# Fixing by hand the order of the last 15 microseconds of a streaming prefix-sum kernel

## The chip, the cores and the metric

The kernel runs on one core of a Trainium2 chip. The metric is the device time in microseconds (us); lower is better. The profile's "span" (first to last instruction) is about 1.7 us shorter than the time.

Names in the profile: PE is the matmul engine TensorE, PEld its weight loads, DVE is VectorE, ACT is ScalarE, POOL is GpSimd, SP is the engine that issues the loads. L218 is a line of the kernel.

## The reference

```python
B, H, W = 4, 4224, 4224          # x: float32
ps   = np.cumsum(np.cumsum(x, axis=1), axis=2)
diag = np.diagonal(ps, axis1=1, axis2=2)
return np.cumsum(diag, axis=1)   # [4, 4224]
```

Only the diagonal of the two-dimensional prefix sum is wanted. Its step from row i-1 to row i is the sum of row i up to the diagonal plus the sum of column i above it. The kernel computes these steps and takes two prefix sums of them.

## The kernel before

Each of the four matrices is read in 33 blocks of 128 rows, 2.1 MB a load, six buffers. For block I, ScalarE sums the rows up to the diagonal block's end, VectorE makes a masked product of the diagonal block and adds the rest to an accumulator, and TensorE turns the masked product and the accumulator's slice into column sums.

```python
for I in range(NB):                                   # NB = 33
    ...
    nc.sync.dma_start(out=xt, in_=x[b, P*I : P*(I+1), :])
    nc.scalar.activation(out=act_scratch[:, 0:P*(I+1)], in_=xt[:, 0:P*(I+1)],
                         func=Copy, accum_out=rp_full[:, I:I+1])          # row sums
    nc.vector.tensor_tensor_reduce(out=du, in0=xt[:, P*I:P*(I+1)], in1=u_strict,
                         ..., accum_out=rp_du[:, I:I+1])                  # masked product
    nc.tensor.matmul(cp_ps[:, I:I+1], lhsT=du, rhs=ones_col, ...)         # column sums
    nc.tensor.matmul(cp_ps[:, I:I+1], lhsT=acc[:, P*I:P*(I+1)], rhs=ones_col, ...)
    nc.vector.tensor_tensor(out=acc[:, P*(I+1):], in0=acc[:, P*(I+1):],
                         in1=xt[:, P*(I+1):], op=add)
```

The last matrix has a tail of its own. The steps of 31 blocks go through the prefix sums while the last two blocks still arrive; the block before the last (31) is loaded in two parts, the last (32) in four chunks; what these two blocks add is put on top by small matmuls.

```python
    # block 31: ScalarE sums columns 0..2304, VectorE the 1792 others
    # block 32: ScalarE sums all four chunks (1408, 1152, 1152, 512 columns)
tt(s31, rp_full[31], rp_du[31], subtract); tt(s31, s31, cp_ps[31], add)
nc.vector.tensor_copy(out=s31mat[:, 31:32], in_=s31)
nc.tensor.matmul(ot_ps[0:32, :], lhsT=s31mat, rhs=ramp_ut, ...)           # rows 0..31
nc.tensor.matmul(ot_ps[32:33, :], lhsT=s31, rhs=ramp_full, ...)
nc.vector.tensor_copy(ot_sb[0:32, :], ot_ps[0:32, :])                     # 32-row copy
nc.gpsimd.dma_start(out=..., in_=ot_sb[0:32, :])
    # five dependent 128x1 additions on VectorE:
    #   pre = part0 + part1; pre += part2; pre2 = pre - rp_du; pre2 += cp_ps; delta = pre2 + part3
nc.tensor.matmul(ot_ps[32:33, :], lhsT=delta, rhs=ramp_ut, ...)           # the last matmul
nc.scalar.copy(ot_sb[32:33, :], ot_ps[32:33, :])
nc.scalar.dma_start(out=..., in_=ot_sb[32:33, :])                         # the last output
```

(`tt` is short for a VectorE addition or subtraction. `s31` holds the steps of block 31, `s31mat` the same as the last column of a matrix of zeros, and `delta` the steps of block 32.) In what order VectorE works through all this is left to the program's scheduler.

## Time and profile before

| before | |
|---|---|
| time, median of 12 runs | 682.93 us (682.72 to 683.09) |
| span of the profiled run | 681.2 us |
| loads | 285.48 MB |
| last chunk told landed (the last of its 16 semaphore updates in the trace) | 673.5 us |
| start of the last matmul | 677.9 us |

The first fence has lines of the page of the kernel before. Slices are fortieths of the span; a digit is the busy share in tenths.

```profile
span 681.2 us, 2484 instructions
DMA  8999999999999999999999999999999999999993
q1 hardware_dynamic: 19584, 285.48, 98.6%
q8 instruction: 4, 0.07, 0.0%
q14 instruction: 9, 0.07, 0.0%
DMA 82%; DVE 9%; ACT 5%; PE 2%; issue 1%; SPq 0%; DVEq 0%; ACTq 0%
```

The DMA engines are full from the second slice to the last but one: the loads bind. (The last line is the chain of waits by engine: 82% of it is DMA.) At about 429 GB/s the bytes alone take 665 us. A change of the tail can therefore touch only what lies after the stream.

The second fence is the timeline of the tail of the kernel before: start, duration, engine, line, operation; in brackets the idle time just before and what ended it.

```profile
671.37 2.00 DVE L218 TENSOR_REDUCE rp_parts<-xt 128x1 f32<-128x1792 f32 x1
673.30 0.27 DVE L238 CUSTOM_DVE_ANT_0 du<-xt,u_strict 128x128 f32<-128x128 f32 x1
673.63 0.59 PE L248 MATMUL cp_ps<-ones_col,du 128*128 128x1 f32 x2 [1.50 <-DVE rp_du L238]
673.78 0.27 DVE L238 CUSTOM_DVE_ANT_0 du<-xt,u_strict 128x128 f32<-128x128 f32 x1
674.55 0.18 ACT L190 ACTIVATION_READ_ACCUMULATOR act_scratch<-xt 128x1 f32 x1
675.54 0.15 DVE L299 TENSOR_TENSOR s<-s,cp_ps 128x1 f32<-128x1 f32 x1 [1.41 <-PE cp_ps L258]
675.94 0.42 PE L306 MATMUL ot_ps<-ramp_ut,s31mat 128*32 128x128 f32 x1 [0.43 <-DVE s31mat L305]
676.62 0.28 DVE L322 COPY ot_sb<-ot_ps 32x128 f32<-32x128 f32 x1 [0.74 <-PE ot_ps L314]
677.72 0.16 DVE L346 TENSOR_TENSOR delta<-pre,rp_parts 128x1 f32<-128x1 f32 x1
677.94 0.59 PE L354 MATMUL ot_ps<-ramp_ut,delta 128*1 128x128 f32 x2 [1.37 <-DVE delta L346]
678.56 0.26 ACT L362 COPY ot_sb<-ot_ps 1x128 f32<-1x128 f32 x1 [3.83 <-PE ot_ps L354]
678.85 0.50 ACTq L363 DMA_DIRECT2D out_dram<-ot_sb  x1
```

Both masked products (the two L238 lines) stand behind the 2.00 us reduce, although their data had landed earlier. TensorE sits idle for them, and VectorE then sits idle 1.41 us for the column sums. ScalarE had its last row sum at 674.7 (L190). From there to 677.9 everybody waits for a chain of small operations.

### The profile page before, as it was taken

The numbers are of one execution on the slowest core, as the hardware profiler recorded it, in microseconds if no ns is written. First come the engines' busy times: TensorE is split into PE (matmuls) and PEld (weight loads), VectorE is DVE, ScalarE is ACT, GpSimd is POOL, SyncE is SP. The second block draws the span as 40 slices with busy tenths as digits, with TensorE's granted clock in tenths as the row PEclk, the third lists the DMA queues.
The fourth block names the chain that finished last, engine by engine and source line by source line (L and its number), as shares of the span: only waits on it lengthen the run. The fifth ranks groups of instructions, "written<-read, shape, count | busy, mean of one in ns | idle before, by whom it ended". The sixth has DMA issues, their size and how long they took to land.

```text
span 681.2 us, 2484 instructions
## 1 busy us (share of the span) xinstructions
PE 146.1 (21%) x590; PEld 129.2 (19%) x590; DVE 330.3 (48%) x440; ACT 279.1 (41%) x272; POOL 4.0 (1%) x16
## 2 busy tenths in 40 slices
PE   0121121121321211211232211212123112112124
PEld 0121121121211211211221111212112112112112
DVE  3876553221587664421177755533118866544213
ACT  1122344567312333555712223445661123345565
POOL 1000000000000000000000000000000000000000
DMA  8999999999999999999999999999999999999993
GB/s 365 433 429 429 429 429 428 428 429 428 428 428 430 429 428 427 429 429 429 427 430 429 429 427 427 429 429 429 429 429 429 429 428 429 429 429 429 429 422 136
DMA packets 19727, 285.69 MB, mean 419 GB/s; under 512 B 2256, under 2 KB 2306, under 8 KB 2946
## 3 DMA queue, kind: packets, MB, share of 16 engines
q1 hardware_dynamic: 19584, 285.48, 98.6%
q8 instruction: 4, 0.07, 0.0%
q0 software_dynamic: 128, 0.07, 0.0%
q14 instruction: 9, 0.07, 0.0%
q10 hardware_dynamic: 2, 0.00, 0.0%
HBM read 285.47 MB, written 0.07 MB: 419 GB/s over the span
## 4 chain that ended last, share of the span: by engine, by line
DMA 82%; DVE 9%; ACT 5%; PE 2%; issue 1%; SPq 0%; DVEq 0%; ACTq 0%
DMA xt<-in_x_dram 82%; DVE acc L273 6%; ACT act_scratch L230 5%; DVE acc L269 1%; DVE du L238 1%; PE cs_ps L110 0%; PE ot_ps L114 0%; PE cs_ps L101 0%; DVE rp_parts L218 0%; DVE p_sb L96 0%; DVE a_sb L96 0%; PE p_ps L106 0%; PE p_ps L119 0%; SPq L185 0%; PE cp_ps L248 0%
## 5 line engine op out<-in xcount | busy, mean ns | idle before, releaser
L230 ACT ACTIVATE act_scratch<-xt 128x128 bf16<-128x128 f32 (+10 forms) x130 | 258.9, 1991 | 393.9 <-DMA xt<-in_x_dram 393.9
L273 DVE TENSOR_TENSOR acc<-acc,xt 128x3968 f32<-128x3968 f32 (+30 forms) x124 | 283.5, 2286 | 0.0
L238 DVE CUSTOM_DVE_ANT_0 du<-xt,u_strict 128x128 f32<-128x128 f32 x132 | 38.4, 291 | 318.4 <-DMA xt<-in_x_dram 318.4
L248 PE MATMUL cp_ps<-ones_col,du 128*128 128x1 f32 x264 | 77.3, 362 | 514.5 <-DVE rp_du L238 514.4
L248 PEld LDWEIGHTS cp_ps<-ones_col,du 128*128 128x128 f32 x264 | 66.2, 311 | 527.2 <-DVE rp_du L238 517.5
L258 PE MATMUL cp_ps<-ones_col,acc 128*128 128x1 f32 x256 | 72.4, 352 | 0.0
L258 PEld LDWEIGHTS cp_ps<-ones_col,acc 128*128 128x128 f32 x256 | 69.9, 333 | 0.0
L230 ACT ACTIVATION_READ_ACCUMULATOR act_scratch<-xt 128x1 f32 x130 | 24.2, 186 | 0.0
L238 DVE DVE_READ_ACCUMULATOR2_ANT rp_du<- 128x1 f32 x132 | 10.8, 82 | 0.1
L269 DVE COPY acc<-xt 128x4096 f32<-128x4096 f32 x4 | 9.1, 2276 | 0.0
L281 DVE TENSOR_TENSOR s_sb<-rp_full,rp_du 128x33 f32<-128x33 f32 x3 | 0.6, 195 | 10.5 <-ACT act_scratch L230 10.5
L101 PE MATMUL cs_ps<-s_sb,u_incl 128*128 128x33 f32 x8 | 2.5, 412 | 11.7 <-DVE s_sb L284 8.9
L190 ACT ACTIVATE act_scratch<-xt 128x1152 bf16<-128x1152 f32 (+2 forms) x4 | 4.3, 1074 | 1.2 <-DMA xt<-in_x_dram 1.1
L290 POOL DMA_DIRECT2D out_dram<-ot_sb x3 | 1.7, 573 | 513.3 <-DVE rp_du L238 513.3
L96 DVE COPY a_sb<-a_ps 33x1 f32<-33x1 f32 x8 | 1.2, 151 | 6.6 <-PE a_ps L103 3.4
L101 PEld LDWEIGHTS cs_ps<-s_sb,u_incl 128*128 128x128 f32 x8 | 2.0, 312 | 12.0 <-DVE s_sb L284 9.2
L114 PE MATMUL ot_ps<-u_incl,t_sb 128*33 128x128 f32 x8 | 2.5, 422 | 1.1 <-DVE t_sb L96 1.1
L110 PE MATMUL cs_ps<-p_sb,u_incl 1*128 1x33 f32 x8 | 2.5, 408 | 1.1 <-DVE p_sb L96 1.1
L123 PE MATMUL ot_ps<-u_incl,p_sb 1*33 1x128 f32 x8 | 2.5, 417 | 0.3 <-DVE p_sb L96 0.3
L96 DVE COPY p_sb<-p_ps 1x33 f32<-1x33 f32 x8 | 1.4, 181 | 2.3 <-PE p_ps L106 1.4
L110 PEld LDWEIGHTS cs_ps<-p_sb,u_incl 1*128 1x128 f32 x8 | 2.0, 307 | 1.8 <-DVE p_sb L96 1.8
L96 DVE COPY t_sb<-cs_ps 128x33 f32<-128x33 f32 x4 | 0.8, 194 | 2.9 <-PE cs_ps L110 2.9
(52 smaller groups left out, 23.9 us busy)
## 6 DMA issues: line engine op xcount, KB each, us to landing
xt<-in_x_dram SPq DMA_DIRECT2D x130, 2112.0 KB, 27.1
xt<-in_x_dram SPq DMA_DIRECT2D x1, 1152.0 KB, 24.9
xt<-in_x_dram SPq DMA_DIRECT2D x2, 576.0 KB, 24.8
xt<-in_x_dram SPq DMA_DIRECT2D x1, 960.0 KB, 26.8
xt<-in_x_dram SPq DMA_DIRECT2D x1, 704.0 KB, 23.8
xt<-in_x_dram SPq DMA_DIRECT2D x1, 256.0 KB, 20.4
out_dram<-ot_sb POOLq DMA_DIRECT2D x3, 16.5 KB, 5.7
out_dram<-ot_sb POOLq DMA_DIRECT2D x1, 16.0 KB, 1.7
```

The lines of the kernel that those rows point to most:

```text
L96: nc.vector.tensor_copy(dst, src)
L101: nc.tensor.matmul(cs_ps, lhsT=u_incl, rhs=x_sb, start=True, stop=False)
L110: nc.tensor.matmul(cs_ps, lhsT=ones_row, rhs=p_sb, start=False, stop=True)
L114: nc.tensor.matmul(ot_ps, lhsT=t_sb, rhs=u_incl, start=True, stop=False)
L123: nc.tensor.matmul(ot_ps, lhsT=p2_sb, rhs=ones_row, start=False, stop=True)
L190: nc.scalar.activation(out=act_scratch[:, c0:c1], in_=xt[:, c0:c1], func=mybir.ActivationFunctionType.Copy, accum_out=rp_parts[:, ci : ci ...
L230: nc.scalar.activation(out=act_scratch[:, 0 : P * (I + 1)], in_=xt[:, 0 : P * (I + 1)], func=mybir.ActivationFunctionType.Copy, accum_out= ...
L238: nc.vector.tensor_tensor_reduce(out=du, in0=xt[:, P * I : P * (I + 1)], in1=u_strict, scale=1.0, scalar=0.0, op0=mybir.AluOpType.mult, op ...
L248: nc.tensor.matmul(cp_ps[:, I : I + 1], lhsT=du, rhs=ones_col, start=False, stop=False, skip_group_check=True,)
L258: nc.tensor.matmul(cp_ps[:, I : I + 1], lhsT=acc[:, P * I : P * (I + 1)], rhs=ones_col, start=False, stop=False, skip_group_check=True,)
L269: nc.vector.tensor_copy(out=acc[:, P * (I + 1) :], in_=xt[:, P * (I + 1) :])
L273: nc.vector.tensor_tensor(out=acc[:, P * (I + 1) :], in0=acc[:, P * (I + 1) :], in1=xt[:, P * (I + 1) :], op=mybir.AluOpType.add,)
```

## The change

Intent: fix the order of the tail by hand and shorten its last chain. The first 130 loads and all blocks but the last two stay as they are, in the same order on every engine. In the tail, four things change: (1) the masked products and column sums go ahead of the reduce; (2) the last chunk's sum (512 columns) moves from ScalarE to VectorE; (3) the 32-row copy moves from VectorE to ScalarE; (4) the diagonal terms are folded in early, so that four additions are left instead of five, and none stands behind the copy. The split of block 31 moves from column 2304 to 2432. The core of the new tail, cut:

```diff
+        with tc.manual_schedule(engines={DVE, PE, Activation}):
+            for ci, (c0, c1) in enumerate(last_chunks[: NPART - 1]):
+                nc.scalar.activation(... accum_out=rp_parts[:, ci : ci + 1])   # three chunks
+            ...                                          # prefix sums of 31 blocks, pass 1
+            du31 = masked_product(IL, xt31)
+            accumulate(IL, xt31)
+            t_sb = psum_to_sbuf("t_sb", cs_ps)
+            ...
+            duL = masked_product(LAST, xtL)
+            a2_sb = psum_to_sbuf("a2_sb", a2_ps)
+            colsum(IL, du31);  colsum(IL, acc[...]);  colsum(LAST, duL);  colsum(LAST, acc[...])
+            nc.tensor.matmul(p2_ps, lhsT=a2_sb, ...)
+            nc.vector.reduce_sum(out=part(NPART), in_=xt31[:, sp31 : P * (IL + 1)], ...)
+            tt(s31, part(NPART), part(NPART + 1))
+            p2_sb = psum_to_sbuf("p2_sb", p2_ps)
+            nc.tensor.matmul(ot_ps, lhsT=p2_sb, rhs=ones_row, start=False, stop=True)
+            tt(neg2, cp_ps[:, IL : LAST + 1], rp_du[:, IL : LAST + 1], SUB)
+            tt(s31mat[:, 31:32], s31, neg2[:, 0:1])
+            tail_matmul(slice(0, 32), s31mat, ramp_ut, True)
+            tail_matmul(slice(LAST, LAST + 1), s31mat[:, 31:32], ramp_full, False)
+            nc.vector.reduce_sum(out=part(NPART - 1), in_=xtL[:, d0:d1], ...)  # last chunk
+            tt(fold, part(0), part(1))
+            tt(fold, fold, neg2[:, 1:2])
+            tt(rest, fold, part(2))
+            nc.scalar.copy(ot_sb[0:LAST, :], ot_ps[0:LAST, :])                 # 32-row copy
+            tt(delta, rest, part(NPART - 1))
```

More of the change, by code (lines that the diff above doesn't have):

```diff
@@ L11 @@
 BF16 = mybir.dt.bfloat16
+ACT_COPY = mybir.ActivationFunctionType.Copy
+ACT_IDENT = mybir.ActivationFunctionType.Identity
+ADD = mybir.AluOpType.add
+SUB = mybir.AluOpType.subtract
+MULT = mybir.AluOpType.mult
 @with_exitstack
@@ L81 @@
         c_c = rem - c_b
-        sizes = [c_a, c_b, c_c, c_d]
-        assert all(s >= P for s in sizes) and sum(sizes) == W
         last_chunks = [
@@ L89 @@
         ]
-    else:
+        sp31 = min((W * 3 // 5) // P * P, P * (LAST - 1))
+        fast_tail = 0 < sp31 < P * (LAST - 1)
+    if not fast_tail:
         last_chunks = [(0, W)]
+        sp31 = 0
     NPART = len(last_chunks)
@@ L139 @@
         ot_sb = smalls.tile([NB, P], FP32, name="ot_sb")
-        if last_batch:
-            s31mat = smalls.tile([P, 32], FP32, name="s31mat")
-            nc.vector.memset(s31mat, 0.0)
-            pre = smalls.tile([P, 1], FP32, name="pre")
-            pre2 = smalls.tile([P, 1], FP32, name="pre2")
-            delta = smalls.tile([P, 1], FP32, name="delta")
-            s31 = smalls.tile([P, 1], FP32, name="s31")
-        for I in range(NB):
-            if last_batch and I == LAST - 1:
-                nc.vector.tensor_tensor(
-                    out=s_sb[:, 0 : LAST - 1],
-                    in0=rp_full[:, 0 : LAST - 1],
-                    in1=rp_du[:, 0 : LAST - 1],
-                    op=mybir.AluOpType.subtract,
-                )
-                nc.vector.tensor_tensor(
-                    out=s_sb[:, 0 : LAST - 1],
-                    in0=s_sb[:, 0 : LAST - 1],
-                    in1=cp_ps[:, 0 : LAST - 1],
-                    op=mybir.AluOpType.add,
-                )
-                nc.vector.memset(s_sb[:, LAST - 1 : LAST + 1], 0.0)
-                t_sb = cumsum_pass1(s_sb)
-                cumsum_pass2_transposed(t_sb, ot_ps)
-            split31 = last_batch and I == LAST - 1 and NPART > 1
-            chunked = last_batch and I == LAST and NPART > 1
-            split31_cols = min((P * I * 3 // 5) // P * P, P * I) if split31 else 0
-            xt = tiles.tile([P, W], FP32, name="xt")
-            if chunked:
-                for (c0, c1) in last_chunks:
-                    nc.sync.dma_start(
-                        out=xt[:, c0:c1], in_=x[b, P * I : P * (I + 1), c0:c1]
-                    )
-            elif split31 and 0 < split31_cols < W:
-                nc.sync.dma_start(
-                    out=xt[:, 0:split31_cols],
-                    in_=x[b, P * I : P * (I + 1), 0:split31_cols],
-                )
-                nc.sync.dma_start(
-                    out=xt[:, split31_cols:],
-                    in_=x[b, P * I : P * (I + 1), split31_cols:],
-                )
-            else:
-                nc.sync.dma_start(out=xt, in_=x[b, P * I : P * (I + 1), :])
-            act_scratch = scratch.tile([P, W], BF16, name="act_scratch")
-            if chunked:
-                for ci, (c0, c1) in enumerate(last_chunks):
-                    nc.scalar.activation(
-                        out=act_scratch[:, c0:c1],
-                        in_=xt[:, c0:c1],
-                        func=mybir.ActivationFunctionType.Copy,
-                        accum_out=rp_parts[:, ci : ci + 1],
-                    )
-                    if ci == 1:
-                        nc.vector.tensor_tensor(
-                            out=pre,
-                            in0=rp_parts[:, 0:1],
-                            in1=rp_parts[:, 1:2],
-                            op=mybir.AluOpType.add,
-                        )
-                    elif 1 < ci < NPART - 1:
-                        nc.vector.tensor_tensor(
-                            out=pre,
-                            in0=pre,
-                            in1=rp_parts[:, ci : ci + 1],
-                            op=mybir.AluOpType.add,
-                        )
-            elif split31:
-                half = split31_cols
-                nc.scalar.activation(
-                    out=act_scratch[:, 0:half],
-                    in_=xt[:, 0:half],
-                    func=mybir.ActivationFunctionType.Copy,
-                    accum_out=rp_parts[:, NPART : NPART + 1],
-                )
-                nc.vector.reduce_sum(
-                    out=rp_parts[:, NPART + 1 : NPART + 2],
-                    in_=xt[:, half : P * (I + 1)],
-                    axis=mybir.AxisListType.X,
-                )
-                nc.vector.tensor_tensor(
-                    out=rp_full[:, I : I + 1],
-                    in0=rp_parts[:, NPART : NPART + 1],
-                    in1=rp_parts[:, NPART + 1 : NPART + 2],
-                    op=mybir.AluOpType.add,
-                )
-            else:
-                nc.scalar.activation(
-                    out=act_scratch[:, 0 : P * (I + 1)],
-                    in_=xt[:, 0 : P * (I + 1)],
-                    func=mybir.ActivationFunctionType.Copy,
-                    accum_out=rp_full[:, I : I + 1],
-                )
@@ L237, with load_block, diag_and_colparts @@
+        def load_block(I, ranges=None):
+            xt = tiles.tile([P, W], FP32, name="xt")
+            if ranges is None:
+                ranges = [(0, W)]
+            for (c0, c1) in ranges:
+                nc.sync.dma_start(
+                    out=xt[:, c0:c1], in_=x[b, P * I : P * (I + 1), c0:c1]
+                )
+            return xt
+        def diag_and_colparts(I, xt):
             du = dupool.tile([P, P], FP32, name="du")
@@ L243 @@
                 scalar=0.0,
-                op0=mybir.AluOpType.mult,
-                op1=mybir.AluOpType.add,
+                op0=MULT,
+                op1=ADD,
                 accum_out=rp_du[:, I : I + 1],
@@ L265, with accumulate, row_part @@
                 )
-            if I < NB - 1:
-                if I == 0:
-                    nc.vector.tensor_copy(
-                        out=acc[:, P * (I + 1) :], in_=xt[:, P * (I + 1) :]
-                    )
-                else:
-                    nc.vector.tensor_tensor(
-                        out=acc[:, P * (I + 1) :],
-                        in0=acc[:, P * (I + 1) :],
-                        in1=xt[:, P * (I + 1) :],
-                        op=mybir.AluOpType.add,
-                    )
-        if not last_batch:
-            nc.vector.tensor_tensor(
-                out=s_sb, in0=rp_full, in1=rp_du, op=mybir.AluOpType.subtract
-            )
-            nc.vector.tensor_tensor(
-                out=s_sb, in0=s_sb, in1=cp_ps, op=mybir.AluOpType.add
-            )
+        def accumulate(I, xt):
+            if I >= NB - 1:
+                return
+            if I == 0:
+                nc.vector.tensor_copy(
+                    out=acc[:, P * (I + 1) :], in_=xt[:, P * (I + 1) :]
+                )
+            else:
+                nc.vector.tensor_tensor(
+                    out=acc[:, P * (I + 1) :],
+                    in0=acc[:, P * (I + 1) :],
+                    in1=xt[:, P * (I + 1) :],
+                    op=ADD,
+                )
+        def row_part(I, xt):
+            act_scratch = scratch.tile([P, W], BF16, name="act_scratch")
+            nc.scalar.activation(
+                out=act_scratch[:, 0 : P * (I + 1)],
+                in_=xt[:, 0 : P * (I + 1)],
+                func=ACT_COPY,
+                accum_out=rp_full[:, I : I + 1],
+            )
+        n_plain = NB - 2 if last_batch else NB
+        for I in range(n_plain):
+            xt = load_block(I)
+            row_part(I, xt)
+            diag_and_colparts(I, xt)
+            accumulate(I, xt)
+        if not last_batch:
+            nc.vector.tensor_tensor(out=s_sb, in0=rp_full, in1=rp_du, op=SUB)
+            nc.vector.tensor_tensor(out=s_sb, in0=s_sb, in1=cp_ps, op=ADD)
             t_sb = cumsum_pass1(s_sb)
@@ L291 @@
             continue
-        nc.vector.tensor_tensor(
-            out=s31,
-            in0=rp_full[:, LAST - 1 : LAST],
-            in1=rp_du[:, LAST - 1 : LAST],
-            op=mybir.AluOpType.subtract,
-        )
-        nc.vector.tensor_tensor(
-            out=s31,
-            in0=s31,
-            in1=cp_ps[:, LAST - 1 : LAST],
-            op=mybir.AluOpType.add,
-        )
-        nc.vector.tensor_copy(out=s31mat[:, 31:32], in_=s31)
-        nc.tensor.matmul(
-            ot_ps[0:32, :],
-            lhsT=s31mat,
-            rhs=ramp_ut,
-            start=False,
-            stop=True,
-            skip_group_check=True,
-        )
@@ L314 @@
-        nc.tensor.matmul(
-            ot_ps[LAST : LAST + 1, :],
-            lhsT=s31,
-            rhs=ramp_full,
-            start=False,
-            stop=False,
-            skip_group_check=True,
-        )
-        nc.vector.tensor_copy(ot_sb[0:LAST, :], ot_ps[0:LAST, :])
-        nc.gpsimd.dma_start(
-            out=out_by_block[b, 0:LAST, :], in_=ot_sb[0:LAST, :]
-        )
-        if NPART == 1:
-            base_ap = rp_full[:, LAST : LAST + 1]
-        elif NPART == 2:
-            base_ap = rp_parts[:, 0:1]
-        else:
-            base_ap = pre
@@ L333 @@
-        nc.vector.tensor_tensor(
-            out=pre2,
-            in0=base_ap,
-            in1=rp_du[:, LAST : LAST + 1],
-            op=mybir.AluOpType.subtract,
-        )
-        nc.vector.tensor_tensor(
-            out=pre2,
-            in0=pre2,
-            in1=cp_ps[:, LAST : LAST + 1],
-            op=mybir.AluOpType.add,
-        )
-        if NPART > 1:
-            nc.vector.tensor_tensor(
-                out=delta,
-                in0=pre2,
-                in1=rp_parts[:, NPART - 1 : NPART],
-                op=mybir.AluOpType.add,
-            )
-        else:
-            delta = pre2
+        IL = LAST - 1
@@ new lines @@
+        s31mat = smalls.tile([P, 32], FP32, name="s31mat")
+        nc.vector.memset(s31mat, 0.0)
+        neg31 = smalls.tile([P, 1], FP32, name="neg31")
+        vs31 = smalls.tile([P, 1], FP32, name="vs31")
+        s31 = smalls.tile([P, 1], FP32, name="s31")
+        negL = smalls.tile([P, 1], FP32, name="negL")
+        fold = smalls.tile([P, 1], FP32, name="fold")
+        rest = smalls.tile([P, 1], FP32, name="rest")
+        delta = smalls.tile([P, 1], FP32, name="delta")
+        xt31 = load_block(IL, [(0, sp31), (sp31, W)])
@@ new lines, with masked_product @@
+        xtL = load_block(LAST, last_chunks)
+        nc.vector.memset(s_sb[:, IL : LAST + 1], 0.0)
+        act_scratch = scratch.tile([P, W], BF16, name="act_scratch")
+        nc.scalar.activation(
+            out=act_scratch[:, 0:sp31],
+            in_=xt31[:, 0:sp31],
+            func=ACT_COPY,
+            accum_out=rp_parts[:, NPART + 1 : NPART + 2],
+        )
+        neg2 = smalls.tile([P, 2], FP32, name="neg2")
+        def masked_product(I, xt):
+            du = dupool.tile([P, P], FP32, name="du")
+            nc.vector.tensor_tensor_reduce(
+                out=du, in0=xt[:, P * I : P * (I + 1)], in1=u_strict,
+                scale=1.0, scalar=0.0, op0=MULT, op1=ADD,
+                accum_out=rp_du[:, I : I + 1],
+            )
+            return du
@@ new lines, in colsum, with tail_matmul, tt @@
+        def colsum(I, lhsT):
+            nc.tensor.matmul(
+                cp_ps[:, I : I + 1], lhsT=lhsT, rhs=ones_col,
+                start=False, stop=False, skip_group_check=True,
+            )
+        def tail_matmul(rows, lhsT, rhs, stop):
+            nc.tensor.matmul(
+                ot_ps[rows, :], lhsT=lhsT, rhs=rhs,
+                start=False, stop=stop, skip_group_check=True,
+            )
+        def tt(o, a, c, op=ADD):
+            nc.vector.tensor_tensor(out=o, in0=a, in1=c, op=op)
@@ new lines, in part @@
+        def part(k):
+            return rp_parts[:, k : k + 1]
+        with tc.manual_schedule(
+            engines={mybir.EngineType.DVE, mybir.EngineType.PE, mybir.EngineType.Activation}
+        ):
+            for ci, (c0, c1) in enumerate(last_chunks[: NPART - 1]):
+                nc.scalar.activation(
+                    out=act_scratch[:, c0:c1],
+                    in_=xtL[:, c0:c1],
+                    func=ACT_COPY,
+                    accum_out=rp_parts[:, ci : ci + 1],
+                )
+            tt(s_sb[:, 0:IL], rp_full[:, 0:IL], rp_du[:, 0:IL], SUB)
+            tt(s_sb[:, 0:IL], s_sb[:, 0:IL], cp_ps[:, 0:IL])
+            cs_ps = psum_ph2.tile([P, NB], FP32, name="cs_ps")
+            nc.tensor.matmul(cs_ps, lhsT=u_incl, rhs=s_sb, start=True, stop=False)
+            a_ps = psum_ph2.tile([NB, 1], FP32, name="a_ps", tag="aux_ps")
+            nc.tensor.matmul(a_ps, lhsT=s_sb, rhs=ones_col, start=True, stop=True)
+            a_sb = psum_to_sbuf("a_sb", a_ps)
+            p_ps = psum_ph2.tile([1, NB], FP32, name="p_ps", tag="aux_ps")
+            nc.tensor.matmul(
+                p_ps, lhsT=a_sb, rhs=u_strict[0:NB, 0:NB], start=True, stop=True
+            )
+            p_sb = psum_to_sbuf("p_sb", p_ps)
+            nc.tensor.matmul(cs_ps, lhsT=ones_row, rhs=p_sb, start=False, stop=True)
+            du31 = masked_product(IL, xt31)
+            accumulate(IL, xt31)
+            t_sb = psum_to_sbuf("t_sb", cs_ps)
+            nc.tensor.matmul(ot_ps, lhsT=t_sb, rhs=u_incl, start=True, stop=False)
+            a2_ps = psum_ph2.tile([NB, 1], FP32, name="a2_ps", tag="aux_ps")
+            nc.tensor.matmul(a2_ps, lhsT=t_sb, rhs=ones_col, start=True, stop=True)
+            duL = masked_product(LAST, xtL)
+            a2_sb = psum_to_sbuf("a2_sb", a2_ps)
+            colsum(IL, du31)
+            colsum(IL, acc[:, P * IL : P * (IL + 1)])
+            colsum(LAST, duL)
+            colsum(LAST, acc[:, P * LAST : P * (LAST + 1)])
+            p2_ps = psum_ph2.tile([1, NB], FP32, name="p2_ps", tag="aux_ps")
+            nc.tensor.matmul(
+                p2_ps, lhsT=a2_sb, rhs=u_strict[0:NB, 0:NB], start=True, stop=True
+            )
+            nc.vector.reduce_sum(
+                out=part(NPART),
+                in_=xt31[:, sp31 : P * (IL + 1)],
+                axis=mybir.AxisListType.X,
+            )
+            tt(s31, part(NPART), part(NPART + 1))
[5 more added lines that the diff above has]
+            tail_matmul(slice(LAST, LAST + 1), s31mat[:, 31:32], ramp_full, False)
+            d0, d1 = last_chunks[NPART - 1]
+            nc.vector.reduce_sum(
+                out=part(NPART - 1), in_=xtL[:, d0:d1], axis=mybir.AxisListType.X
+            )
+            tt(fold, part(0), part(1))
[3 more added lines that the diff above has]
+            tt(delta, rest, part(NPART - 1))
@@ L354 @@
+        nc.gpsimd.dma_start(out=out_by_block[b, 0:LAST, :], in_=ot_sb[0:LAST, :])
         nc.tensor.matmul(
```

## The prediction

> **What bounds the kernel now.** The input stream. The page's queue part shows 285.48 MB on the load queue, 98.6% of 16 engines' span; its slices show 427 to 433 GB/s from the second slice on, and the chain of waits gives DMA 82%. (The Trainium skill, "Perfetto Trace Analysis", section "Roofline", puts the 16 DMA engines of a single active core at about 435 GB/s; this trace agrees, 429.) At 429 GB/s the bytes alone take 665 us of the 681.2 us span. The change doesn't touch the 130 whole-block loads; the instruction order of both programs is the same on every engine until the last two blocks. So only what lies after the stream can move. By the packet records the last input packet ends at 673.0 us, and its landing is told at 673.5. The tail after it is 7.7 us, 1.1% of the span: under 2% is certain unless the stream itself breaks.
>
> **The tail now** (timeline of the last 15 us). VectorE works in an order the scheduler chose: the small prefix copies first, then a 1792-wide reduce (671.4 to 673.4, 2.00 us), and only then both masked products of the last two blocks (673.3, 673.8). The four column-sum matmuls therefore run 673.6 to 675.5, s31 at 675.5, its two tail matmuls 675.9 to 676.6, the 32-row copy on VectorE 0.28, then five dependent 128x1 additions from 676.8 to 677.9, about 0.2 us each, the last matmul 677.94, the ScalarE copy 678.56, and the output's issue at 678.85. ScalarE had finished the last chunk at 674.7, so all from there is this chain. Issue to the end of the span: 2.3 us, unchanged.
>
> **After the change, same durations.** s_sb until p_sb stays where it was (666.9 to 669.05). The masked products fit into waits of VectorE at 669.1 and 670.1 (chunk of the last block told by then), so the column sums run at 670.7 to 672.4. The reduce, now 1664 wide (estimate 1.87 us by width), runs 670.95 to 672.8; s31, p2 copy, neg2, s31mat to 673.65. The 512-wide reduce moves from ScalarE (0.61 + 0.19) to VectorE: estimate 0.65, from 673.65 to 674.3. Four additions of 0.2: delta ready at 675.1. Meanwhile the p2 matmul and two tail matmuls end at about 674.6, and ScalarE's 32-row copy ends at 674.9, just before delta, which matters because the last matmul now waits for it too. Last matmul 675.2, ScalarE copy 675.8, issue 676.1. Against 678.85 that is 2.7 us. The 32-row output, issued by GpSimd after 675.0, took 1.7 us to land, and stays hidden.
>
> The removed and added work is nearly equal in size (DVE gains the 0.65 reduce, loses the 0.28 copy and one addition); the gain is order, not work. All of it is on the critical path, since nothing else is left to do after the stream.
>
> **Predicted: 680.2 us**, 8 in 10 between 679.2 and 681.4. Faster by over 2%: 0.005; within 2%: 0.99; slower: 0.005.
>
> **What would show it.** Right: slices and GB/s unchanged to the last; last input packet near 673.0; column sums of the last two blocks start near 670.7; the last ScalarE copy near 675.8; the span near 678.4; VectorE nearly gapless from 671 to 675 and the chain of waits at its end going through its two reduces. Wrong: the column sums still after 673; the last matmul waiting on ScalarE's 32-row copy by over 0.3 us; the issue later than 677.
>
> **What would make it wrong.** From 670.8 to 673.0 only one of the 16 DMA engines still works (DMA share 0.06): if this straggler ends a microsecond earlier or later, because the split at column 2432 instead of 2304 changes packet sizes, the time follows, as VectorE's last reduce waits for it. A small-operation latency 0.1 us longer in each of some eight dependent steps would eat 0.8 us.

## The result, and the profile after

The median is 680.32 us (679.75 to 680.52, 10 runs) against 682.93 us (12 runs): 2.6 us or 0.4% less. The ratio is 0.9961, 95% interval 0.9952 to 0.9970. The prediction was 680.2 us.

Lines of the page of the changed kernel:

```profile
span 678.6 us, 2479 instructions
DMA  8999999999999999999999999999999999999994
q1 hardware_dynamic: 19584, 285.48, 99.0%
DMA 85%; DVE 8%; ACT 5%; PE 1%; issue 1%; SPq 0%; DVEq 0%; ACTq 0%
```

The stream is the same. The timeline of its tail, columns as above:

```profile
669.30 0.27 DVE L252 CUSTOM_DVE_ANT_0 du<-xt,u_strict 128x128 f32<-128x128 f32 x1
670.40 0.29 DVE L252 CUSTOM_DVE_ANT_0 du<-xt,u_strict 128x128 f32<-128x128 f32 x1
670.98 0.59 PE L260 MATMUL cp_ps<-ones_col,du 128*128 128x1 f32 x2
671.16 1.87 DVE L316 TENSOR_REDUCE rp_parts<-xt 128x1 f32<-128x1664 f32 x1
673.49 0.16 DVE L272 TENSOR_TENSOR s31mat<-s,neg 128x1 f32<-128x1 f32 x1
673.86 0.69 DVE L329 TENSOR_REDUCE rp_parts<-xt 128x1 f32<-128x512 f32 x1 [0.21 <-DMA xt<-in_x_dram]
674.69 0.25 ACT L335 COPY ot_sb<-ot_ps 32x128 f32<-32x128 f32 x1 [0.23 <-PE ot_ps L266]
675.10 0.16 DVE L272 TENSOR_TENSOR delta<-rest,rp_parts 128x1 f32<-128x1 f32 x1
675.41 0.59 PE L338 MATMUL ot_ps<-ramp_ut,delta 128*1 128x128 f32 x2 [0.77 <-DVE delta L272]
676.03 0.26 ACT L346 COPY ot_sb<-ot_ps 1x128 f32<-1x128 f32 x1 [1.09 <-PE ot_ps L338]
676.32 0.49 ACTq L347 DMA_DIRECT2D out_dram<-ot_sb  x1
```

The column sums start at 671.0 instead of 673.6, beside the reduce instead of behind it. s31mat is ready at 673.65 instead of 675.9. VectorE now waits 0.21 us for the last chunk: the tail has become so short that the landing of the last load is what its end hangs on. The chain of waits of the changed kernel shows the same: it is DMA until 673.83, then the 512-column reduce, the additions and the last matmul.

```profile
653.48 20.36 DMA xt<-in_x_dram
673.86 0.69 DVE rp_parts L329
675.10 0.17 DVE delta L272
675.41 0.60 PE ot_ps L338 x2
676.03 0.26 ACT ot_sb L346
```

A useful measure for all runs below, since the landing itself moves from run to run, is the time from "last chunk told landed" to "start of the last matmul". It was 677.94 - 673.49 = 4.45 us before and 675.41 - 673.83 = 1.58 us after. The rest, from the last matmul to the end of the span, is unchanged at 3.2 us. Of this, 2.3 us lie between the start of the last output's issue and the end (678.85 to 681.2 before, 676.32 to 678.6 after). The Trainium skill, "DMA: Bandwidth & Descriptors", section "Anatomy of one DMA", puts the fixed cost of a DMA issued from GpSimd at about 2.0 us; here GpSimd's 32-row output landed 1.7 us after its issue. The last output is issued by ScalarE: its landing was told 1.1 us after the start of the issue (at 677.41), and the span ended 1.2 us after that.

### The profile page after: what moved, and what is told of

Its sections match the earlier page's. It is cut to its first block, busy times and chain, and to the rows that moved or that the text cites. A ratio compares the mean times of both kernels' runs of the same rounds, so it can differ in the third digit from the quotient of the medians.

```text
span 678.6 us, 2479 instructions
## 1 busy us (share of the span) xinstructions
PE 145.9 (22%) x590; PEld 129.3 (19%) x590; DVE 330.3 (49%) x438; ACT 278.9 (41%) x271; POOL 4.0 (1%) x16
## 4 chain that ended last, share of the span: by engine, by line
DMA 85%; DVE 8%; ACT 5%; PE 1%; issue 1%; SPq 0%; DVEq 0%; ACTq 0%
DMA xt<-in_x_dram 85%; DVE acc L195 6%; ACT act_scratch L204 5%; DVE acc L191 1%; DVE du L159 1%; PE cs_ps L116 0%; PE ot_ps L120 0%; PE cs_ps L107 0%; SPq L152 0%; DVE p_sb L102 0%; DVE rp_parts L329 0%; DVE a_sb L102 0%; PE ot_ps L338 0%; PE p_ps L112 0%; PE p_ps L125 0%
## 5 line engine op out<-in xcount | busy, mean ns | idle before, releaser
L281 ACT ACTIVATE act_scratch<-xt 128x1152 bf16<-128x1152 f32 (+1 forms) x3 | 3.7, 1234 | 1.0 <-DMA xt<-in_x_dram 0.9
L242 ACT ACTIVATE act_scratch<-xt 128x2432 bf16<-128x2432 f32 x1 | 2.2, 2212 | 0.0
## 6 DMA issues: line engine op xcount, KB each, us to landing
xt<-in_x_dram SPq DMA_DIRECT2D x130, 2112.0 KB, 27.1
```

The source lines that it names most:

```text
L242: nc.scalar.activation(out=act_scratch[:, 0:sp31], in_=xt31[:, 0:sp31], func=ACT_COPY, accum_out=rp_parts[:, NPART + 1 : NPART + 2],)
L281: nc.scalar.activation(out=act_scratch[:, c0:c1], in_=xtL[:, c0:c1], func=ACT_COPY, accum_out=rp_parts[:, ci : ci + 1],)
```

## The experiments

Twelve kernels were run; all gave correct results. "Landed" is when the last chunk was told landed, "last matmul" when it started, both in the profiled run. Each was timed in five rounds with the kernel before on the same chip, the 120-row run in three.

| run | median us | ratio to before (95%) | landed | last matmul | between |
|---|---|---|---|---|---|
| before | 682.93 | | 673.49 | 677.94 | 4.45 |
| after | 680.32 | 0.9961 (0.9952-0.9970) | 673.83 | 675.41 | 1.58 |
| order undone | 681.87 | 0.9985 (0.9972-0.9997) | 673.68 | 677.01 | 3.33 |
| last chunk on ScalarE | 680.11 | 0.9960 (0.9948-0.9973) | 673.67 | 675.25 | 1.58 |
| copy on VectorE | 680.46 | 0.9963 (0.9951-0.9976) | 673.62 | 675.20 | 1.58 |
| order alone | 680.79 | 0.9968 (0.9954-0.9982) | 673.54 | 675.87 | 2.33 |
| order and chain | 680.29 | 0.9962 (0.9948-0.9975) | 673.65 | 675.14 | 1.49 |
| half of TensorE's instructions | 680.91 | 0.9972 (0.9959-0.9984) | 674.39 | 675.97 | 1.58 |
| new tail, first try | 680.77 | 0.9969 (0.9955-0.9982) | 673.54 | 675.61 | 2.07 |
| first try and half of TensorE's | 681.80 | 0.9984 (0.9971-0.9998) | 674.71 | 676.88 | 2.17 |
| 120 and 8 rows | 683.88 | 1.0010 (0.9995-1.0025) | 677.36 | 679.00 | 1.64 |
| fewer VectorE instructions | 678.63 | 0.9938 (0.9925-0.9952) | 672.15 | 673.73 | 1.58 |
| new tail, mended | 680.44 | 0.9965 (0.9952-0.9977) | 673.41 | 674.90 | 1.49 |
| mended and fewer VectorE | 678.88 | 0.9942 (0.9929-0.9954) | 672.26 | 673.71 | 1.45 |

The intervals are about as wide as 1.8 us, so a difference of half a microsecond between two runs is not settled by them. Where the text below rests on so small a difference, it leans on the timeline, and says whether the single times overlap.

### What of the change was worth what

Theory A: the order is the gain. Rival B: the work moved between VectorE and ScalarE is.

**Order undone.** The changed kernel with products and column sums behind the reduce. (The last chunk's reduce and the first addition also move ahead, into VectorE's wait for the column sums; this is not in the cut.)

```diff
-            du31 = masked_product(IL, xt31); accumulate(IL, xt31)     # ahead of t_sb
-            duL = masked_product(LAST, xtL)                           # ahead of a2_sb
-            colsum(IL, ...) x2;  colsum(LAST, ...) x2                 # ahead of the reduce
+            p2_sb = psum_to_sbuf("p2_sb", p2_ps); ...
             nc.vector.reduce_sum(out=part(NPART), in_=xt31[:, sp31 : P * (IL + 1)], ...)
+            du31 = ...; accumulate(...); duL = ...; colsum x4
```

> The changed kernel with one thing undone: the two masked products and the four column-sum matmuls are put back behind the 1664-wide reduce; the last chunk's sum stays on VectorE and the 32-row copy on ScalarE. Theory A (the gain is the order: the column sums no longer wait for the reduce): the reduce runs 671.5 to 673.4, the column sums 673.7 to 675.5, the tail matmuls from 675.9, and the last issue comes at about 678, so the span is 1.7 us longer than the changed kernel's (about 682.0 us, ratio to before near 0.9985). Rival B (the gain is the work moved between VectorE and ScalarE, not the order): it stays within 0.4 us of 680.3.

Measured: 681.87 us, 1.55 us worse than the changed kernel, with no overlap of single times (681.58 and more against 680.52 and less). Its timeline shows the same waits as before the change:

```profile
671.58 1.86 DVE L311 TENSOR_REDUCE rp_parts<-xt 128x1 f32<-128x1664 f32 x1
673.71 0.59 PE L260 MATMUL cp_ps<-ones_col,du 128*128 128x1 f32 x2 [1.37 <-DVE rp_du L252]
675.61 0.16 DVE L272 TENSOR_TENSOR neg<-cp_ps,rp_du 128x2 f32<-128x2 f32 x1 [0.81 <-PE cp_ps L260]
677.01 0.58 PE L338 MATMUL ot_ps<-ramp_ut,delta 128*1 128x128 f32 x2 [0.36 <-ACT ot_sb L335]
```

**Last chunk back on ScalarE.**

```diff
-            for ci, (c0, c1) in enumerate(last_chunks[: NPART - 1]):
+            for ci, (c0, c1) in enumerate(last_chunks):
-            nc.vector.reduce_sum(out=part(NPART - 1), in_=xtL[:, d0:d1], ...)
```

> The changed kernel with the sum of the last chunk (512 columns) put back on ScalarE. Theory A: ScalarE ends the chunk before at 674.3, sums the last chunk until 675.1, then copies the 32 rows until 675.4, and the last matmul waits for that copy: 0.3 us longer than the changed kernel, 680.6 us. Rival B (this move is most of the gain): over 1.5 us longer.

**32-row copy back on VectorE.**

```diff
-            nc.scalar.copy(ot_sb[0:LAST, :], ot_ps[0:LAST, :])
+            nc.vector.tensor_copy(ot_sb[0:LAST, :], ot_ps[0:LAST, :])
```

> The changed kernel with the 32-row copy put back on VectorE, ahead of the last addition. Theory A: the copy's 0.28 us is added to VectorE's last chain and nothing else: 680.6 us. Rival B: over 1.5 us longer.

Neither costs anything that these runs can show: 680.11 and 680.46 us, and 1.58 us from landing to the last matmul in both, as in the changed kernel. Both of my estimates of 0.3 us were misses. When the last chunk is summed on ScalarE, VectorE is free to do two of its additions ahead of it, and the two effects cancel. When the copy is on VectorE, it starts 0.06 us ahead of the end of the addition before it, and the last addition ahead of the copy's end, so it adds 0.12 us between the last two additions (0.31 from start to start instead of 0.19), and the last matmul then starts 0.19 us after the last addition instead of 0.31.

**Order alone.** Both put back, the five additions behind the copy, and the split at 2304:

```diff
+        sp31 = 2304
+            for ci, (c0, c1) in enumerate(last_chunks):               # all four on ScalarE
+            nc.vector.tensor_copy(ot_sb[0:LAST, :], ot_ps[0:LAST, :]) # ahead of the additions
             tt(fold, part(0), part(1))
-            tt(fold, fold, neg2[:, 1:2])
-            tt(rest, fold, part(2))
+            tt(fold, fold, part(2))
+            tt(rest, fold, rp_du[:, LAST : LAST + 1], SUB)
+            tt(rest, rest, cp_ps[:, LAST : LAST + 1])
             tt(delta, rest, part(NPART - 1))
```

> Only the order of the change: masked products and column sums ahead of the reduce, but the last chunk summed on ScalarE, the 32-row copy on VectorE ahead of five dependent additions, and the split of the block before the last at column 2304, all as in the kernel before. Theory A: tail matmuls end at 674.7, copy until 675.0, five additions until 676.1, so 0.9 us longer than the changed kernel: 681.2 us, which is 1.8 of the 2.6 us gained. Rival B: no faster than before by more than 0.5 us.

Measured: 680.79 us, so the order alone gives 2.1 of the 2.6 us. Its five runs (680.61 to 680.83) all lie above the ten of the changed kernel (679.75 to 680.52), and its timeline shows where the rest is: the copy and all five additions follow one another.

```profile
674.56 0.28 DVE L328 COPY ot_sb<-ot_ps 32x128 f32<-32x128 f32 x1 [1.04 <-PE ot_ps L266]
674.77 0.14 DVE L272 TENSOR_TENSOR fold<-rp_parts 128x1 f32<-128x1 f32 x1
675.66 0.16 DVE L272 TENSOR_TENSOR delta<-rest,rp_parts 128x1 f32<-128x1 f32 x1
675.87 0.58 PE L335 MATMUL ot_ps<-ramp_ut,delta 128*1 128x128 f32 x2 [1.36 <-DVE delta L272]
```

**Order and chain.** To close the sum, one more kernel differs from "order alone" in four lines: the additions are the changed kernel's, the copy stands ahead of the last one only. Both pieces of work stay on their old engines.

```diff
-            nc.vector.tensor_copy(ot_sb[0:LAST, :], ot_ps[0:LAST, :])
             tt(fold, part(0), part(1))
-            (three additions as above)
+            tt(fold, fold, neg2[:, 1:2]);  tt(rest, fold, part(2))
+            nc.vector.tensor_copy(ot_sb[0:LAST, :], ot_ps[0:LAST, :])
             tt(delta, rest, part(NPART - 1))
```

> The changed kernel's order and its shorter chain of additions (the diagonal terms folded in early, the 32-row copy not ahead of all additions), but with both pieces of work where they were before: the last chunk summed on ScalarE, the 32-row copy on VectorE, the split at column 2304. It differs from the run of the order alone only in four lines. Put back singly, the two moves cost nothing (680.1 and 680.5 against 680.3), yet the order alone leaves 0.5 us. Theory A2 (the rest is the chain of additions behind the copy, the moves are worth nothing): 680.2 us, within 0.25 of the changed kernel. Rival B2 (the moves are needed together): 680.7 us or more, as the order alone.

Measured: 680.29 us, 1.49 us from landing to the last matmul. It was run on another chip. The copy now stands in a wait, and one addition follows it:

```profile
674.65 0.28 DVE L331 COPY ot_sb<-ot_ps 32x128 f32<-32x128 f32 x1 [0.18 <-PE ot_ps L266]
674.93 0.16 DVE L272 TENSOR_TENSOR delta<-rest,rp_parts 128x1 f32<-128x1 f32 x1
675.14 0.58 PE L334 MATMUL ot_ps<-ramp_ut,delta 128*1 128x128 f32 x2 [0.54 <-DVE delta L272]
```

Rival B falls: within what the runs resolve (the medians of the three runs lie within 0.25 us of the changed kernel's), order and the shorter chain are the whole gain, and the two moves of work are worth nothing, singly or together. The two parts don't add up exactly: the order alone gains 2.1 us, but taken out of the whole change it costs 1.55 us, probably because "order undone" fills part of VectorE's wait with the last chunk's reduce and additions.

### The last load: one of 16 DMA engines is late

After the change the end hangs on the landing. The prediction had named a straggler. The DMA share by microsecond in the changed kernel (stretch, its length, busy time of PE, PEld, DVE, ACT and POOL, granted clock, DMA share, GB/s):

```profile
671.00:672.00 1.00, 1.00 (x6) 1.00 (x6) 0.91 (x2) 1.00 (x3) 0.00 (x0) 1.00 0.06 23
672.00:673.00 1.00, 1.00 (x6) 0.84 (x6) 1.00 (x1) 1.00 (x2) 0.00 (x0) 1.00 0.07 27
```

A share of 0.06 is one engine of 16. Each load's semaphore is raised once by each of the 16 engines when its part has landed (the Trainium skill, "DMA: Bandwidth & Descriptors", section "Why a DMA increments its semaphore by 16 and not by 1"; the trace has 16 such updates for each load). Sorted, those of the last chunk were told at these times (us):

```
before: 669.1 669.2 669.3 669.5 669.5 669.5 669.6 669.7 669.8 670.7 670.9 671.0 671.1 671.2 671.2  673.5
after:  669.3 669.4 669.5 669.5 669.5 669.5 669.6 669.6 669.7 670.8 670.9 671.0 671.3 671.4 671.4  673.8
```

Fifteen engines are done by 671.4, and the last chunk waits 2.3 to 2.4 us for one. Loads of the first 80 us show no such gap (0.1 us). Following the gap from load to load, it grows in steps, the last two of 1.0 us each, and some of them fall beside instruction transfers (queues 8 and 14 on the page: 16 KB and 8 KB each).

**Half of TensorE's instructions** (theory L: the late engine carries TensorE's instructions):

```diff
+            if I >= 1:
+                nc.vector.tensor_tensor(out=du, in0=du, in1=acc[:, P * I : P * (I + 1)], op=ADD)
             nc.tensor.matmul(cp_ps[:, I : I + 1], lhsT=du, rhs=ones_col, ...)
-            if I >= 1:
-                nc.tensor.matmul(cp_ps[:, I : I + 1], lhsT=acc[:, P * I : P * (I + 1)], ...)
```

> The changed kernel with one column-sum matmul per block instead of two in all blocks but the last two: VectorE adds the accumulator's 128 columns into the masked product first (0.27 us a block), so TensorE executes about half its instructions. It tests why one of the 16 DMA engines ends 2.3 us after the other 15. In both traces that distance grew by 1.0 us just when the third and fourth of four 16 KB instruction transfers (1.0 to 1.1 us each, at 125, 267, 414 and 557 us) ran. Theory L (one DMA engine also carries TensorE's instructions and never catches up): the 16 KB transfers fall from 4 to 2, the last engine's distance to the last but one to under 1.2 us, and the last chunk is told landed 1 to 2.3 us earlier. The time gains little by itself, 0 to 0.6 us against 680.3, since VectorE's 1664-wide reduce (to 673.0) and ScalarE's third chunk then hold the tail. Rival M (that engine is slow for another reason): the distance stays at 2.2 to 2.4 us.

Measured: 680.91 us, worse. The 16 KB transfers did fall to two, but the gap grew to 3.0 us. Theory L fell. The expectation had also misread the traces: the steps of 1.0 us came at 392.7 and 550.1 us, beside 8 KB transfers, and not with the 16 KB transfers at 414.3 and 556.3. From the page of this run:

```profile
PE 92.0 (14%) x338; PEld 75.4 (11%) x338; DVE 355.9 (52%) x564; ACT 278.9 (41%) x271; POOL 4.0 (1%) x16
q14 instruction: 10, 0.08, 0.0%
q8 instruction: 2, 0.03, 0.0%
```

VectorE executes 564 instructions here instead of 438. In the traces before, after and of this run, each step of the late engine falls on an 8 KB instruction transfer that took 325 to 333 ns. The delay below is the late engine's, measured against the fourth engine to finish the same load:

```
run                    such transfers begin at (us)         the engine's delay before -> after, on the load that ends next
before                 83.5, 241.0, 392.7, 550.1            0.6 -> 1.3, 1.3 -> 2.3, 2.3 -> 3.3, 3.2 -> 4.2
half of TensorE's      73.4, 182.3, 327.0, 454.2, 576.3     0.6 -> 1.2, 1.2 -> 2.2, 2.2 -> 3.2, 3.2 -> 4.2, 4.2 -> 5.1
```

(In the kernel before, another engine was the last between 131 and 241 us, 1.9 us behind the fourth. It had been set back by the 16 KB transfer at 124.7 us; the 1.3 in the second pair is the last but one.) The other nine transfers of that trace, of both sizes, do the same to other engines: after each, one of the 16 sorted times is later by 0.6 us or more and stays so. They seem to be what puts six more engines 0.9 us and more behind the first nine in the list above. The late engine is the last because four steps add up on it.

The transfers of 325 to 333 ns come every 155 us before and every 126 us here, roughly in proportion to VectorE's instructions (440 before the change and 564 here), and not to TensorE's, which were nearly halved. Theory N: these are VectorE's instructions; each 8 KB sets the engine that carries them back by 1 us, and since the engine's queue is never empty (a load takes 27.1 us from issue to landing and one lands every 5.05 us), it never catches up.

**New tail, first try, and both.** At the same time I tried a tail that starts from other loads: VectorE sums the first 1536 columns of block 31 early, VectorE and ScalarE sum the last two chunks side by side, the last partial sums enter by matmuls of their own, and all 33 rows leave in one output.

```diff
+        sp31 = 12 * P                      # VectorE sums columns 0..1536 of block 31, ahead of s_sb
+            for ci in (0, 1, 3): nc.scalar.activation(...)    # ScalarE: chunks 0, 1, 3
+            tt(du31, du31, acc[...]); colsum(IL, du31)        # one column sum a block
+            tt(fold, part(0), part(1)); tt(fold, fold, neg2[:, 1:2])
+            nc.vector.reduce_sum(out=part(2), ...)            # VectorE: chunk 2
+            tail_matmul(LAST, fold); tail_matmul(LAST, part(2)); last matmul: part(3)
+        nc.scalar.copy(ot_sb, ot_ps);  nc.scalar.dma_start(out=out_by_block[b], in_=ot_sb)
```

> An attempt at a better tail, load sizes of the last block unchanged: VectorE sums the first 1536 columns of the block before the last while it waits for ScalarE; VectorE sums the third chunk and ScalarE the fourth at the same time; masked products and accumulator are added on VectorE ahead of one column sum; the last partial sums go into the last row by matmuls of their own instead of additions; one copy and one output of 33 rows. Theory A: what is left after the landing (third chunk told at 673.0, fourth at 673.7) is one reduce of 1.3 us, one matmul 0.6, copy and issue: issue at 675.6 instead of 676.3, so about 679.7 us. If the tail were bound by anything ahead of the landing, it would not improve on 680.3.

> Both. Theory L with A: the landing 1 to 2 us earlier is now worth most of itself: 678.3 us, range 677.8 to 679.0. Rival M: the same as the new tail alone.

Measured: 680.77 and 681.80 us, both misses. VectorE's sum of the third chunk stood behind two additions that wait for ScalarE and started at 673.83, though its data was told at 672.9; and the matmul of part 2, which ends last, stood ahead of part 3's. With half of TensorE's instructions the landing was later still (674.71).

**120 and 8 rows.** Could the late engine be left out of the last loads?

```diff
-            for (c0, c1) in ranges:
-                nc.sync.dma_start(out=xt[:, c0:c1], in_=x[b, P * I : P * (I + 1), c0:c1])
+            for ci, (c0, c1) in enumerate(ranges):
+                for (r0, r1) in [(0, 120), (120, P)] if ci >= 2 else [(0, P)]:
+                    nc.sync.dma_start(out=xt[r0:r1, c0:c1], in_=x[b, P * I + r0 : P * I + r1, c0:c1])
```

> The changed kernel with the last two chunks each loaded as rows 0 to 119 and rows 120 to 127. The Trainium skill (DMA: Bandwidth & Descriptors, section on the semaphore's increment by 16) says that 120 rows go to the 15 lowest-numbered engines and 8 rows to the 8 lowest. If the late engine is the highest-numbered one, the last landing comes 1.5 us earlier or more; if it is any other, the landing comes at the same time or 0.1 to 0.4 us later and the time is the same or worse by as much.

Measured: 683.88 us, 1 us worse than before the change. The last landing, of the last chunk's 8-row load, came at 677.36, 3.5 us later, far more than the 0.1 to 0.4 us that I expected. Even the first chunk of this block, loaded whole, was late: its row sum started at 673.08 instead of 670.39. And the split did not leave the late engine out: the 15 data updates of the last chunk's 120-row load end with 674.48 and 677.18, and the eight of its 8-row load with 674.66 and 677.36, so in both one engine is 2.7 us behind the others. Such a split is harmful here; why it costs so much was not found out.

**Fewer VectorE instructions** (theory N). GpSimd, idle otherwise, makes the masked block with two selects; the second, in place, clears what ScalarE must not sum. VectorE keeps one addition a block.

```diff
+        def mask_on_pool(I, xt):
+            du = dupool.tile([P, P], FP32, name="du")
+            blk = xt[:, P * I : P * (I + 1)]
+            nc.gpsimd.affine_select(out=du,  in_=blk, fill=0.0, base=-1, pattern=[[1, P]],  channel_multiplier=-1, ...)
+            nc.gpsimd.affine_select(out=blk, in_=blk, fill=0.0, base=0,  pattern=[[-1, P]], channel_multiplier=1, ...)
+            return du
         for I in range(n_plain):
             xt = load_block(I)
+            du = None if (last_batch and I == n_plain - 1) else mask_on_pool(I, xt)
             row_part(I, xt)
-            diag_and_colparts(I, xt)
+            diag_and_colparts(I, xt, du)   # no VectorE product where du is given
```

> The changed kernel with the masks of all blocks but the last three made on GpSimd (two selects of 128x128 a block, the second in place ahead of ScalarE's row sum), so VectorE executes 185 instructions instead of 438. The run with half of TensorE's instructions refuted theory L: the last engine's distance grew to 3.0 us. In all nine traces each step of about 1.0 us of that engine falls on an 8 KB instruction transfer of 325 to 333 ns, four in the kernels before and after (near 83, 241, 393 and 550 us), five in the run whose VectorE executes 131 instructions more. Theory N (those are VectorE's instructions, and each delays the engine that carries them by 1 us for good): at most two such transfers, the last engine is 0.7 us or less behind the last but one, the last chunk is told landed 1 to 2 us earlier than 673.8, and the whole tail moves with it: 678.8 us, range 678.2 to 679.4. Rival M (the engine is slow for another reason) : distance 2 us or more, and 680.3 or more. A loss from GpSimd and VectorE blocking each other would show as ScalarE starting late in the last ten blocks.

Measured: 678.63 us, ratio 0.9938, the fastest of all, and 1.7 us below the changed kernel. From its page:

```profile
span 676.9 us, 2738 instructions
PE 146.2 (22%) x590; PEld 129.4 (19%) x590; DVE 303.3 (45%) x184; ACT 278.8 (41%) x271; POOL 339.7 (50%) x274
q1 hardware_dynamic: 19584, 285.48, 99.2%
```

Its trace has two transfers of 325 ns (154.8 and 437.8 us) instead of four. The last chunk is told landed at 672.15 instead of 673.83, the last engine 0.54 us behind the last but one, and the tail, unchanged at 1.58 us, moves with it:

```profile
672.18 0.69 DVE L347 TENSOR_REDUCE rp_parts<-xt 128x1 f32<-128x512 f32 x1 [0.24 <-DMA xt<-in_x_dram]
673.73 0.59 PE L356 MATMUL ot_ps<-ramp_ut,delta 128*1 128x128 f32 x2 [0.80 <-DVE delta L290]
```

One caution: the run also gives GpSimd 258 more instructions, so it is not VectorE's count alone that changed. The trace bears on this: it has four 8 KB transfers of 309 to 312 ns that the changed kernel's lacks (78.4, 241.2, 402.7 and 564.2 us). After each, one of the sorted times is later by 0.4 to 0.7 us, on what looks like one other engine, which is the last in the end. So GpSimd's instructions, whose they seem to be, are not free either. What carries theory N is that VectorE's count was moved in both directions and the late engine's gap followed it each time, while halving TensorE's count did not shrink the gap. No run moved VectorE's count alone. That the transfers belong to VectorE is inferred from their rate; the trace doesn't name their owner.

The selects on GpSimd are not free. Alone, a 128x128 select took 0.28 us at the kernel's start; here the first of each pair took 2.06 us on average, about as long as VectorE's addition beside it:

```profile
L162 POOL TENSOR_SCALAR_AFFINE_SELECT du<-xt 128x128 f32<-128x128 f32 x129 | 265.7, 2060 | 291.4 <-DMA xt<-in_x_dram 240.0 <-ACT act_scratch L220 34.1 <-DVE rp_du L157 8.8
```

The Trainium skill, "SBUF — State Buffer", section "SBUF: two separate sides", says that a VectorE operation with two SBUF inputs and a GpSimd operation that reads SBUF exclude each other for the whole instruction; this trace agrees (at 302.9 us a select took 1.22 us beside an addition of 1.09). It costs nothing here because both engines have room within the 5.05 us of a block, and the last three blocks keep the old form.

**New tail, mended, and both.** The third chunk's sum ahead of the additions, the last matmuls in the order in which their inputs come:

```diff
-            tt(fold, part(0), part(1)); tt(fold, fold, neg2[:, 1:2])
+            tt(fold, part(0), neg2[:, 1:2])
             nc.vector.reduce_sum(out=part(2), ...)
+            tail_matmul(LAST, fold); tail_matmul(LAST, part(1)); tail_matmul(LAST, part(3)); last: part(2)
```

> The new tail, mended: in the first try VectorE's sum of the third chunk stood behind two additions that waited for ScalarE (it started at 673.8, not 673.1), and the last row's matmuls were in the wrong order. Now the sum starts at 673.4 and ends at 674.7, only its matmul (0.6), the copy and the issue (675.7) follow. Theory A: 679.9 us, 0.4 less than the changed kernel. If the output of 33 rows in one transfer takes as long as in the first try (2.5 us from issue to end instead of 2.3), at most that is gained.

> Both together. Theory N with A: 678.4 us, range 677.8 to 679.2; rival M: as the mended tail alone.

Measured: 680.44 and 678.88 us, both 0.5 us over the expected value and no better than the changed kernel's tail with the same stream (680.32 and 678.63). The last matmul starts 1.49 us after the landing, 0.1 us sooner, but the single output of 33 rows takes 2.45 us from issue (675.85) to the end of the span (678.3) instead of 2.3. The tail of the change is already about as short as these rearrangements make it.

## Why the prediction was right

- **The bound.** Right. Slices and bytes of the stream are the same in both pages; only the tail moved.
- **The column sums come out from behind the reduce.** Right: predicted at 670.7, measured 670.98; s31mat predicted at 673.65, measured 673.65; and undoing the order gives 1.55 us back. That s31mat agrees to the hundredth is luck: the reduce began 0.2 us later than predicted (671.16 against 670.95), and the small operations after it took 0.62 us instead of 0.85.
- **Sizes.** The 1664-wide reduce was estimated at 1.87 us and took 1.87; the 512-wide one 0.65 and took 0.69. Delta was predicted ready at 675.1 and was ready at 675.26 (675.10 plus 0.16). The last ScalarE copy was predicted at 675.8, and started at 676.03; the issue 676.1, and was 676.32; the span 678.4, and was 678.6. All are late by 0.2, as the last chunk was told landed 0.34 us later in this profile (673.83 against 673.49), and the last reduce now waits for it.
- **What ends the chain.** Partly wrong. The prediction had the chain of waits going "through its two reduces", with the short one following the long one at once. Measured, it goes from the landing into the short one; the long one was done early enough. The prediction's own caution, the late DMA engine, is what the tail now stands on.
- **"The gain is order, not work."** Right about the work: moving the last chunk and the copy back costs nothing, together or singly. But "order" lumped two things: the column sums (2.1 us by the order alone, 1.55 us by undoing it) and the chain of additions behind the copy (0.5 us, shown by "order alone" against "order and chain").
- **The hidden output.** Right: the 32-row output was issued at 675.23 and never held the end.

## What to carry to other kernels

Where a stream binds a kernel, as here, look for what reordering can win after its last byte; measure every variant from the landing of the last load, because the landing itself moves by some tenths from run to run. In such a tail, put what another engine waits for ahead of long work that nobody waits for, and fold early terms early; which engine does a small piece mattered less here. Then look at the last load engine by engine: here one late DMA engine cost 2.3 us, nearly as much as the whole change gained, and fewer VectorE instructions over the whole kernel won 1.7 us of it.

## What the Trainium skill lacked or had wrong

- "Runtime: NRT & Kernel Launch", section "Instruction fetch mechanics", says that instruction memory is refilled in 16 KiB blocks and that crossing a boundary is "mostly hidden". Here most instruction transfers were of 8 KB (9 of 13 on the kernel's page), and they were not hidden from the stream: the four of 325 to 333 ns each set one DMA engine back by 0.7 to 1.0 us for good, and at the end it was 2.3 us behind the last but one.
- "DMA: Bandwidth & Descriptors" does not say that the engines of a long stream fall apart step by step, one engine at each instruction transfer. Within one load they finished within 0.7 us of one another at the start and within 4.4 us at the end.
- The same page, section "Why a DMA increments its semaphore by 16 and not by 1", gives a rule by which 120 rows use 15 engines. The trace agrees (one update came at once, at issue, and 15 with the data), but no page says what it costs: the last landing came 3.5 us later than with whole loads.
- "SBUF — State Buffer" gives the exclusion of VectorE and GpSimd as a rule; the number here is 2.06 us on average for a select that takes 0.28 us alone.
